# Turning three tiles on VectorE and through transfers instead of on TensorE, in a one-core decoder layer

## The chip, the core and the metric

The kernel runs on one core of a Trainium2 chip. A core has five engines that work side by side, each through its own queue of instructions in order: TensorE (PE in the profile, with its weight loads as PEld), VectorE (DVE), ScalarE (ACT), GpSimd (POOL) and SyncE (SP), whose queue here does little but issue transfers (DMAs) between the chip's memory and the core's. The metric is the time of one execution on the device in microseconds (us); lower is better. Of several executions the median counts.

## What is computed

One layer of a hybrid decoder over 256 tokens of width 1024, all in float32:

```python
def reference(x, ...):
    mix = hybrid_mixer(x, ...)
    x = layer_norm(ALPHA * x + mix, ln1_g, ln1_b)
    ffn = conv_gated_mlp(x, w_up, conv_ffn, w_down)
    return layer_norm(ALPHA * x + ffn, ln2_g, ln2_b)

def hybrid_mixer(x, ...):
    proj = x @ w_in + b_in                 # q,k,v,o,i,f of the memory; q,k,v of the attention; two gates
    qk = silu(causal_dwconv(concat(q_m, k_m), conv_qk))
    h_m = mlstm_chunkwise(q_m, k_m, v_m, i_m, f_m)          # 4 heads x 256
    y_a = sigmoid(o_m) * head_norm(h_m, mlstm_norm)
    y_b = moba_attention(q_b, k_b, v_b, rel_bias)           # 8 heads x 128
    merged = sigmoid(g_a) * (y_a @ w_branch_a) + sigmoid(g_b) * (y_b @ w_branch_b)
    return merged @ w_out

def conv_gated_mlp(x, w_up, conv_ffn, w_down):              # 2816 hidden columns
    g, up = split(causal_dwconv(x @ w_up, conv_ffn), 2)
    return (silu(g) * up) @ w_down
```

## The kernel before

**Chunks and slots.** All weights come as chunks of 128 x 2048 numbers (1 MB), in an order written out by hand in `chunk_order` (lines 45 to 58): four of the output gate, then for each of four groups of heads (g = 0 to 3) the chunks qm, qb, km, kb, vm, vb, ga, gb; then the branch chunks wa 0, wa 1, wb 0, wb 1, wa 2, wa 3, wb 2, wb 3; four chunks wo of the output projection; then the up chunks (22) and down chunks (11) of the MLP, mixed. A float32 product is made of three matmuls (`mm3`, line 143): every operand is split into a high part (ACT rounds it, line 94) and the rest (DVE subtracts, line 95). One chunk stands for 48 matmuls of 256 columns, or 24 of 512 for a down chunk.

**The loop** (lines 338 to 375) goes over the chunks; this text calls one turn of it, and the time of its matmuls, a slot. In slot s the code hands out, in this order: to ACT and DVE what is due (`elem_work`, line 381: the evacuation of the previous chunk's result, extra pieces from `side_elem`, and the split of chunk s+2, put between them where the list has a `None`; `mixed` can reorder the list); to SP the load of chunk s+5; to PE the matmuls of chunk s and then the pieces of `side_pe`. Every engine works its queue strictly in the order of the code. A tile that is given out again waits until all readers of its former content are done: raw chunks, high parts and low parts each have three buffers, and the results of the chunks share three banks of the accumulator memory (PSUM), "main", while five banks, "side", serve the rest.

**Groups.** In each group a head pair's memory output `yt` has tokens on the partitions and must be turned so that features are there (`yah`, `yal`: the operands of wa). For groups 0 to 2 `turn` (line 636) does this: DVE transposes 32 x 32 blocks into a spare tile, SP writes that to the chip's memory (line 644), and four loads bring it back (line 648); only then does `el_y` (line 755) split it. For the last group PE turns it: `pe_y` (line 748), four transposes at the end of slot gb 3, whose result in PSUM `el_y` reads. The two attention logits of a group are turned by `turn` in all four groups (`turn(0)` and `turn(1)`), cast by `el_t`, and used by `pe_o` (line 817); `el_o` (line 830) writes `ybh`, `ybl`, the operands of wb. For the last group `pe_o` stands at the end of slot wa 0 and `el_o` in slot wa 1.

**MLP.** The first two up chunks are multiplied with the tokens on the partitions (`step_up`, lines 1032 to 1047), since the second half of the tokens is normalised late. So their results have to be turned: `copy` brings them to `tu`, and `back` (line 1055), run by PE in the middle of chunk up 2, makes eight transposes into PSUM, `ps_upT`. `up_evac` (line 1076) is the evacuation of an up chunk: `conv` scales twice on ACT (line 1088) and adds two taps on DVE (line 1092, four instructions), `gate` applies Silu on ACT (line 1099), multiplies on DVE (line 1103) and splits into `hh` and `hl`. The evacuations of up 0, up 1 and up 2 are woven together (line 1073). Down chunk d needs the results of up chunks 2d and 2d + 1. Up chunks from number 6 on are split in one piece of 2048 columns, the others in two of 1024 (line 116).

Of the kernel before, what the change touches and what calls it, by code (L numbers as in the profile page):

```python
# [10 lines left out]
F32 = mybir.dt.float32  # L11
# [7 lines left out]
P = 128  # L19
S = 256  # L20
D = 1024
KT = D // P
# [22 lines left out]
def chunk_order():  # L45
# [7 lines left out]
    order += [("up", i) for i in range(4)]  # L53
    for d in range(8):
        order += [("dn", d), ("up", 2 * d + 4), ("up", 2 * d + 5)]
# [17 lines left out]
class Kernel:  # L73
# [69 lines left out]
    def mm3(self, ps, ah, al, bh, bl, start, stop, first=None, only=(0, 1, 2)):  # L143

        a = (ah if first is None else first, ah, al)
        b = (bh, bl, bh)
        for i in only:
            self.nc.tensor.matmul(ps, a[i], b[i], start=start and i == 0, stop=stop and i == 2)  # L148

# [30 lines left out]
    def run(self):  # L180
# [132 lines left out]
        for s, (kind, i) in enumerate(self.order):  # L313
            if kind == "qm":
# [5 lines left out]
        self.mrows = dram.tile([4, S], F32, name="mrows")  # L320
        self.flip = [[dram.tile([m, P, n * P], F32, name=f"flip{g}{i}")
                      for i, (m, n) in enumerate(((1, 3), (1, 3), (2, 2))[:3 if g < NG - 1 else 2])] for g in range(NG)]
# [15 lines left out]
        for s, (kind, i) in list(enumerate(self.order))[4:]:  # L338
# [3 lines left out]
            if s == first["wa"] + 1:  # L342
# [21 lines left out]
            parts = [] if late else self.split_parts(s + 2)  # L364
            if s == first["wa"] - 1:
                self.kept, parts = parts[-1], parts[:-1]
            self.elem_work(s, parts)
# [268 lines left out]
    def turn(self, t, d):  # L636
# [3 lines left out]
        tmp = self.ap.tile([P, 4 * P], F32, tag="turn", name="turn", bufs=2)[:, 0:n * P]  # L640
# [3 lines left out]
        self.nc.sync.dma_start(d.rearrange("m p f -> p m f"), tmp.rearrange("p (m f) -> p m f", m=m))  # L644
        t = t.rearrange("p c s -> p (c s)").rearrange("p (k f) -> p k f", k=4 * m)
# [4 lines left out]
    def group_schedule(self, g):  # L650
# [97 lines left out]
        def pe_y():  # L748
            psy = self.ps_side([P, 2, S], f"psy{g}")
            for j in range(2):  # L750
                for t in range(2):
                    nc.tensor.transpose(psy[:, j, t * P:(t + 1) * P], st["yt"][:, t, j * P:(j + 1) * P], self.ident)
            st["psy"] = psy

        def el_y():
            for j in range(2):
# [3 lines left out]
                if last:  # L760
                    y = st["psy"][:, j, :]
                else:
                    y = st["yt"].rearrange("p t s -> p (t s)").rearrange("p (m k) -> p m k", k=64)[:, :, 32 * j:32 * j + 32]
                    h, l = (t.rearrange("p (m i) -> p m i", i=32) for t in (h, l))
# [95 lines left out]
        self.mixed[b + 6 + o] = lambda w: ([lambda: el_l(1), lambda: el_e(1), el_n1] + w  # L860
                                           + [lambda: el_l2(1), el_n1b, lambda: turn(1)])
        if last:
            self.mixed[b + 7] = lambda w: [el_n2, lambda: el_t(0)] + w
            at(self.side_pe, 7, pe_y)
            self.mixed[b + 8] = lambda w: [el_y, self.kept, lambda: el_t(1)] + w
        else:
# [3 lines left out]
        at(self.side_pe, 8 + o, pe_o)  # L870
        at(self.side_elem, 9 + o, el_o)
# [19 lines left out]
    def step_wa(self, s, c, *a):  # L891
        nc = self.nc
        ps = self.ps_main(f"ps_wa{c}")
        self.mm_feat(s, ps, self.yah, self.yal)

        def evac():
            ga = self.sg["ga"][:, 2 * c:2 * c + 2, :]
            nc.scalar.activation(ga, ga, AF.Sigmoid)
            nc.vector.tensor_mul(ga, ps, ga)
        self.evac[s] = evac  # L900
# [126 lines left out]
    def step_up(self, s, i, *a):  # L1027
# [4 lines left out]
        if i < 2:  # L1032
# [17 lines left out]

            def copy():
                for j in range(2):
                    self.nc.scalar.copy(tu[:, j], self.pt_up[j])

            def back():
                for j in range(2):
                    ps = self.ps_side([P, 2, S], f"ps_upT{j}")
                    for f in range(2):
                        for t in range(2):
                            self.nc.tensor.transpose(ps[:, f, t * P:(t + 1) * P], tu[:, j, t, f * P:(f + 1) * P],  # L1060
# [260 lines left out]
```

## Time and profile before

| what | us |
|---|---|
| median of 3 runs | 479.17 |
| lowest, highest of them | 478.26, 479.36 |
| the execution that was profiled | 478.69 |
| its span, first to last instruction | 476.7 |
| DVE busy in the span | 368.1 |
| ACT busy in the span | 309.7 |
| bytes moved | 97.35 MB |

The profile is of one execution; its span is 2.0 us shorter than that execution's own time. In the lines shown below, a line of the timeline or of the chain has the start and the length in us, the engine, the line of the code and what it does; "[0.47 <-ACT hh]" says that the engine stood idle 0.47 us before it and what ended that. A group's line ends with the total busy time, and the mean of one in ns. Instructions on one engine overlap a little at their edges (the next starts some 0.1 us before the profile's end of the last), so the step from start to start is what counts where one engine is the limit.

### The profile page before, as it was taken

How to read it: one execution, taken by the hardware profiler on the slowest of the kernel's cores; microseconds unless marked ns; L12 is line 12 of the kernel's file. 1: busy time of each engine (PE TensorE's matmuls, PEld its weight loads, DVE VectorE, ACT ScalarE, POOL GpSimd, SP SyncE). 2: the span in 40 equal slices, each digit the busy share in tenths (PEclk: the TensorE clock that was granted, in tenths of full speed). 3: DMA queues.
4: the chain of work that ended last, by engine and by line, in shares of the span. 5: the costliest groups of instructions: out<-in, count | busy, mean ns of one | idle time of the engine just before them, and what ended most of it. 6: DMA issues, size and time to landing. Idle time of an engine off the chain costs nothing.

```text
span 476.7 us, 9493 instructions
## 1 busy us (share of the span) xinstructions
PE 469.3 (98%) x3788; PEld 454.8 (95%) x3788; DVE 368.1 (77%) x644; ACT 309.7 (65%) x540; POOL 37.4 (8%) x74
## 2 busy tenths in 40 slices
PE   8999999999999999999999999999999999999994
PEld 6999999999999999999999999999999999999984
DVE  4786979597869786986685898879668666778876
ACT  5669878597859786977663623765555545556871
POOL 0316501000200020010100001000000000000000
PEclk9999999999999999999999999999999999999999
DMA  7985665775666567655967472736564545456202
GB/s 232 324 298 180 212 239 162 222 276 195 173 239 247 193 171 253 234 169 177 368 243 260 148 294 88 268 101 252 184 236 170 206 178 192 171 214 219 89 0 89
DMA packets 28958, 97.35 MB, mean 204 GB/s; under 512 B 10581, under 2 KB 15585, under 8 KB 19697
## 3 DMA queue, kind: packets, MB, share of 16 engines
q1 hardware_dynamic: 27682, 92.51, 55.3%
q0 software_dynamic: 1232, 4.24, 2.7%
q8 instruction: 29, 0.48, 0.4%
q14 instruction: 15, 0.12, 0.1%
HBM read 93.31 MB, written 3.42 MB: 203 GB/s over the span
## 4 chain that ended last, share of the span: by engine, by line
PE 98%; DVE 0%; ACT 0%; DVEq 0%; issue 0%; ACTq 0%
PE ps_up L148 25%; PE ffn L148 13%; PE ps_ga L148 5%; PE ps_kb L148 5%; PE ps_vm L148 5%; PE mix L148 5%; PE ps_km L148 5%; PE ps_gb L148 5%; PE ps_wa L148 5%; PE ps_vb L148 5%; PE ps_wb L148 5%; PE ps_qm L148 5%; PE ps_qb L148 5%; PE ps_o0a L427 1%; PE ps_o0b L427 1%; PE psn L148 1%
## 5 line engine op out<-in xcount | busy, mean ns | idle before, releaser
L95 DVE TENSOR_TENSOR wl<-raw,wh 128x1024 fp32r<-128x1024 f32 (+4 forms) x147 | 180.0, 1261 | 26.8 <-ACT wh L94 24.5
L94 ACT CAST wh<-raw 128x1024 fp32r<-128x1024 f32 (+4 forms) x147 | 151.8, 1077 | 9.3 <-DMA raw<-in_wst_dram 4.0
L148 PE MATMUL ps_up<-x1h,wl 128*128 128x256 f32 x320 | 88.5, 276 | 0.0
L148 PE MATMUL ps_up<-x1h,wh 128*128 128x256 f32 x320 | 88.4, 276 | 0.0
L148 PE MATMUL ps_up<-x1l,wh 128*128 128x256 f32 x320 | 88.4, 276 | 0.0
L148 PEld LDWEIGHTS ps_up<-x1l,wh 128*128 128x128 f32 x320 | 60.1, 188 | 0.4
L148 PEld LDWEIGHTS ps_up<-x1h,wh 128*128 128x128 f32 x320 | 60.1, 188 | 0.3
L148 PEld LDWEIGHTS ps_up<-x1h,wl 128*128 128x128 f32 x320 | 60.1, 188 | 0.0
L1092 DVE SCALAR_TENSOR_TENSOR cu<-ps_up,vec,cu 128x255 f32<-128x255 f32 (+1 forms) x80 | 33.1, 476 | 20.1 <-ACT cu L1088 20.1
L148 PE MATMUL ffn<-wh,hl 128*128 128x512 f32 (+2 forms) x94 | 35.5, 378 | 0.0
L148 PE MATMUL ffn<-wl,hh 128*128 128x512 f32 (+2 forms) x94 | 35.5, 377 | 0.0
L148 PE MATMUL ffn<-wh,hh 128*128 128x512 f32 (+2 forms) x94 | 35.3, 375 | 0.0
L94 ACT CAST hh<-cu 128x256 fp32r<-128x256 f32 x22 | 8.9, 406 | 40.4 <-DVE cu L1103 40.4
L1088 ACT ACTIVATE cu<-ps_up,vec 128x256 f32<-128x256 f32 x40 | 16.7, 470 | 22.0 <-PE ps_up L148 22.0
L148 PEld LDWEIGHTS ffn<-wh,hl 128*128 128x128 f32 x94 | 17.7, 188 | 3.2
L148 PEld LDWEIGHTS ffn<-wl,hh 128*128 128x128 f32 x94 | 17.7, 188 | 3.1
L148 PEld LDWEIGHTS ffn<-wh,hh 128*128 128x128 f32 x94 | 17.7, 188 | 3.0
L990 POOL TENSOR_TENSOR rs<-rs,mhalf 128x1 f32<-128x1 f32 x3 | 2.1, 700 | 230.2 <-DVE rs L989 230.2
L148 PE MATMUL ps_ga<-xth,wh 128*128 128x256 f32 x64 | 18.0, 281 | 0.0
L148 PE MATMUL mix<-wh,mgh 128*128 128x256 f32 x64 | 17.8, 279 | 0.0
L148 PE MATMUL ps_wa<-yah,wh 128*128 128x256 f32 x64 | 17.8, 277 | 0.0
L148 PE MATMUL ps_kb<-xth,wl 128*128 128x256 f32 x64 | 17.7, 277 | 0.0
(344 smaller groups left out, 1476.6 us busy)
## 6 DMA issues: line engine op xcount, KB each, us to landing
raw<-in_wst_dram SPq DMA_DIRECT2D x72, 1024.0 KB, 4.9
raw<-in_wst_dram SPq DMA_DIRECT2D x10, 512.0 KB, 6.7
raw<-in_wst_dram SPq DMA_DIRECT2D x8, 256.0 KB, 4.5
lnrow<-in_rows_dram POOLq DMA_DIRECT2D x4, 512.0 KB, 6.9
flip<-turn SPq DMA_DIRECT2D x8, 192.0 KB, 3.2
lg<-flip SPq DMA_DIRECT2D x32, 48.0 KB, 2.0
xraw<-in_xt_dram SPq DMA_DIRECT2D x8, 128.0 KB, 4.0
toe<-table POOLq DMA_DIRECT2D x4, 256.0 KB, 4.7
```

The source lines that it names most:

```text
L94: self.nc.scalar.copy(wh, raw)
L95: self.nc.vector.tensor_sub(wl, raw, wh.bitcast(F32))
L148: self.nc.tensor.matmul(ps, a[i], b[i], start=start and i == 0, stop=stop and i == 2)
L427: mm(ps[t], x[:, k, t * P:(t + 1) * P], w, start=start and k == 0, stop=stop and k == KT - 1)
L990: nc.gpsimd.tensor_tensor(st["rs"], st["rs"], self.mhalf[:, 0:1], op=ALU.pow)
L1088: act.activation(cu[:, j, :], ps[:, j, :], AF.Copy, scale=tap(2, j))
L1092: v.scalar_tensor_tensor(cu[:, j, o:], ps[:, j, :S - o], tap(t, j), cu[:, j, o:], op0=ALU.mult, op1=ALU.add)
```

## The change

Three tiles are no longer turned by PE. The last group's `yt` goes the way of the other groups', through `turn(2)`, and `pe_y` is gone; the order of the last group's pieces over the slots ga, gb and wa 0 is written anew. Since `yt` and the second logits come back from memory in another order, the chunks wa 0 and wa 1 are cut: `mm_rows` runs wa 0 without its last two of eight row blocks (those that need group 3), then wa 1 without them, then the rest of wa 0, then `pe_o`, then the rest of wa 1; `el_o` and both evacuations of wa follow in slot wb 0. The results of up 0 and up 1 are copied to `tu`, turned by DVE into `tv`, written to memory and loaded back into `tu`; `natural` (two copies on ACT for each of the two chunks) brings the blocks into order, and `up_evac` reads `tv`. Their evacuations move to the slots up 4 and up 5. The order of the MLP chunks begins with up 0 to up 5, dn 1, dn 0, up 6, up 7 in place of up 0 to up 3, dn 0, up 4, up 5, dn 1, up 6, up 7; from dn 2 on it is as before.

```diff
--- before.py
+++ after.py
@@ -50,8 +50,8 @@
     for c in (0, 2):
         order += [("wa", c), ("wa", c + 1), ("wb", c), ("wb", c + 1)]
     order += [("wo", c) for c in range(4)]
-    order += [("up", i) for i in range(4)]
-    for d in range(8):
+    order += [("up", i) for i in range(6)] + [("dn", 1), ("dn", 0), ("up", 6), ("up", 7)]
+    for d in range(2, 8):
         order += [("dn", d), ("up", 2 * d + 4), ("up", 2 * d + 5)]
     order += [("up", 20), ("up", 21), ("dn", 8), ("dn", 9), ("dn", 10)]
     assert sum(k == "up" for k, _ in order) == NF and sum(k == "dn" for k, _ in order) == NF // 2
@@ -146,6 +146,14 @@
         b = (bh, bl, bh)
         for i in only:
             self.nc.tensor.matmul(ps, a[i], b[i], start=start and i == 0, stop=stop and i == 2)
+
+    def mm_rows(self, s, ps, xh, xl, ks):
+
+        wh, wl = self.w[s]
+        for j in range(2):
+            for k in ks:
+                a = self.col(s, k * 256 + j * P)
+                self.mm3(ps[j], wh[:, a:a + P], wl[:, a:a + P], xh[:, k, :], xl[:, k, :], k == 0, k == KT - 1)
 
     def mm_feat(self, s, ps, xh, xl, mid=None):
         wh, wl = self.w.pop(s)
@@ -318,8 +326,9 @@
 
         self.table = dram.tile([8, LTOE], F32, name="table")
         self.mrows = dram.tile([4, S], F32, name="mrows")
+        self.flip_up = [dram.tile([1, P, 4 * P], F32, name=f"flipu{j}") for j in range(2)]
         self.flip = [[dram.tile([m, P, n * P], F32, name=f"flip{g}{i}")
-                      for i, (m, n) in enumerate(((1, 3), (1, 3), (2, 2))[:3 if g < NG - 1 else 2])] for g in range(NG)]
+                      for i, (m, n) in enumerate(((1, 3), (1, 3), (2, 2)))] for g in range(NG)]
         self.gates_schedule(bif)
         self.gate_sums()
         self.rel_bias_expand(rel)
@@ -339,7 +348,7 @@
             if s == 10:
                 pre_cm.__exit__(None, None, None)
                 self.open_att(att_cm.__enter__())
-            if s == first["wa"] + 1:
+            if s == first["wa"] + 2:
                 self.elem_work(s)
                 att_cm.__exit__(None, None, None)
                 mix_cm.__exit__(None, None, None)
@@ -361,10 +370,7 @@
 
                 self.fp.tile([P, 24], F32, name="gap")
             late = s == first["up"]
-            parts = [] if late else self.split_parts(s + 2)
-            if s == first["wa"] - 1:
-                self.kept, parts = parts[-1], parts[:-1]
-            self.elem_work(s, parts)
+            self.elem_work(s, [] if late else self.split_parts(s + 2))
             self.load(s + 5)
             if s in (first["wo"], first["wo"] + 1):
                 self.split(s + 4)
@@ -633,15 +639,23 @@
         self.mixed[b + 2] = lambda w: w + [e1b, None, e1c, None, e1d, e1e]
 
 
-    def turn(self, t, d):
+    def turn(self, t, d, tmp=None):
 
         m, _, f = d.shape
         n, w = t.shape[1], t.shape[1] // m
-        tmp = self.ap.tile([P, 4 * P], F32, tag="turn", name="turn", bufs=2)[:, 0:n * P]
+        back = tmp is None
+        if back:
+            tmp = self.ap.tile([P, 4 * P], F32, tag="turn", name="turn", bufs=2)[:, 0:n * P]
         for k in range(m):
             self.nc.vector.transpose(tmp[:, k * f:(k + 1) * f].rearrange("p (b c i) -> p c b i", b=4, i=32),
                                      t[:, k * w:(k + 1) * w].rearrange("p c (b i) -> p c b i", b=4))
         self.nc.sync.dma_start(d.rearrange("m p f -> p m f"), tmp.rearrange("p (m f) -> p m f", m=m))
+        if back:
+            self.turn_in(t, d)
+
+    def turn_in(self, t, d):
+
+        m, _, f = d.shape
         t = t.rearrange("p c s -> p (c s)").rearrange("p (k f) -> p k f", k=4 * m)
         for b in range(4):
             src = d[:, :, b * (f // 4):(b + 1) * (f // 4)].rearrange("m (a j) f -> j m a f", a=4)
@@ -745,23 +759,13 @@
         def turn(i):
             self.turn(st["p", i] if i < 2 else st["yt"].rearrange("p t (j d) -> p (t j) d", j=2), self.flip[g][i])
 
-        def pe_y():
-            psy = self.ps_side([P, 2, S], f"psy{g}")
-            for j in range(2):
-                for t in range(2):
-                    nc.tensor.transpose(psy[:, j, t * P:(t + 1) * P], st["yt"][:, t, j * P:(j + 1) * P], self.ident)
-            st["psy"] = psy
-
         def el_y():
             for j in range(2):
                 c = 2 * g + j
                 gain = self.vec[:, V_NORM + c:V_NORM + c + 1]
                 h, l = self.yah[:, c, :], self.yal[:, c, :]
-                if last:
-                    y = st["psy"][:, j, :]
-                else:
-                    y = st["yt"].rearrange("p t s -> p (t s)").rearrange("p (m k) -> p m k", k=64)[:, :, 32 * j:32 * j + 32]
-                    h, l = (t.rearrange("p (m i) -> p m i", i=32) for t in (h, l))
+                y = st["yt"].rearrange("p t s -> p (t s)").rearrange("p (m k) -> p m k", k=64)[:, :, 32 * j:32 * j + 32]
+                h, l = (t.rearrange("p (m i) -> p m i", i=32) for t in (h, l))
                 a.activation(h, y, AF.Copy, scale=gain)
                 v.scalar_tensor_tensor(l, y, gain, h.bitcast(F32), op0=ALU.mult, op1=ALU.subtract)
 
@@ -857,18 +861,24 @@
         if g == 0:
             at(self.side_elem, 6, lambda: self.floor_exp())
         at(self.side_elem, 5 + o, lambda: turn(0))
-        self.mixed[b + 6 + o] = lambda w: ([lambda: el_l(1), lambda: el_e(1), el_n1] + w
+        if last:
+            self.mixed[b + 6] = lambda w: ([el_n1, el_n1b, lambda: el_l(1), el_n2, lambda: turn(2), None, None,
+                                            lambda: el_e(1)] + w + [lambda: el_l2(1), lambda: turn(1)])
+            self.mixed[b + 7] = lambda w: [lambda: el_t(0)] + w
+            self.mixed[b + 8] = lambda w: [el_y, lambda: el_t(1)] + w
+        else:
+            self.mixed[b + 7] = lambda w: ([lambda: el_l(1), lambda: el_e(1), el_n1] + w
                                            + [lambda: el_l2(1), el_n1b, lambda: turn(1)])
-        if last:
-            self.mixed[b + 7] = lambda w: [el_n2, lambda: el_t(0)] + w
-            at(self.side_pe, 7, pe_y)
-            self.mixed[b + 8] = lambda w: [el_y, self.kept, lambda: el_t(1)] + w
-        else:
             self.mixed[b + 8] = lambda w: [el_n2, lambda: el_t(0), lambda: turn(2)] + w
             self.mixed[b + 9] = lambda w: w[0:1] + [lambda: el_t(1)] + w[1:]
             at(self.side_elem, 10, el_y)
-        at(self.side_pe, 8 + o, pe_o)
-        at(self.side_elem, 9 + o, el_o)
+        if last:
+            self.last_o = pe_o
+            at(self.side_elem, 10, el_o)
+            self.mixed[b + 10] = lambda w: w[-1:] + w[:-1]
+        else:
+            at(self.side_pe, 9, pe_o)
+            at(self.side_elem, 10, el_o)
 
 
     def open_post(self, pp):
@@ -891,13 +901,28 @@
     def step_wa(self, s, c, *a):
         nc = self.nc
         ps = self.ps_main(f"ps_wa{c}")
-        self.mm_feat(s, ps, self.yah, self.yal)
-
-        def evac():
+        ps = [ps[:, j, :] for j in range(2)]
+        if c < 2:
+            ps[1] = self.ps_side([P, 2, 256], f"ps_wa{c}b")[:, 0, :]
+            self.mm_rows(s, ps, self.yah, self.yal, range(KT - 2))
+            if c == 0:
+                self.first_wa = s, ps, c
+                return
+            self.mm_rows(*self.first_wa[:2], self.yah, self.yal, range(KT - 2, KT))
+            self.last_o()
+        self.mm_rows(s, ps, self.yah, self.yal, range(KT - 2 if c < 2 else 0, KT))
+
+        def evac(s, ps, c):
             ga = self.sg["ga"][:, 2 * c:2 * c + 2, :]
             nc.scalar.activation(ga, ga, AF.Sigmoid)
-            nc.vector.tensor_mul(ga, ps, ga)
-        self.evac[s] = evac
+            for j in range(2):
+                nc.vector.tensor_mul(ga[:, j, :], ps[j], ga[:, j, :])
+        done = [(s, ps, c)]
+        if c == 1:
+            done.insert(0, self.first_wa)
+        for t in done:
+            self.w.pop(t[0])
+        self.evac[s] = [lambda t=t: evac(*t) for t in done]
 
     def step_wb(self, s, c, *a):
         nc = self.nc
@@ -1048,30 +1073,32 @@
             del self.w[s - 1], self.w[s]
             tu = self.fp.tile([P, 2, 2, S], F32, name="tu")
 
+            tv = self.fp.tile([P, 2, 2, S], F32, name="tv")
+
             def copy():
+                rows = [tu[:, j].rearrange("p t (f d) -> p (t f) d", f=2) for j in range(2)]
                 for j in range(2):
                     self.nc.scalar.copy(tu[:, j], self.pt_up[j])
-
-            def back():
                 for j in range(2):
-                    ps = self.ps_side([P, 2, S], f"ps_upT{j}")
-                    for f in range(2):
-                        for t in range(2):
-                            self.nc.tensor.transpose(ps[:, f, t * P:(t + 1) * P], tu[:, j, t, f * P:(f + 1) * P],
-                                                     self.ident)
-                    self.pt_up[j] = ps
+                    self.turn(rows[j], self.flip_up[j], tv[:, j].rearrange("p f s -> p (f s)"))
+                for j in range(2):
+                    self.turn_in(rows[j], self.flip_up[j])
+
+            def natural(j):
+                src = tu[:, j].rearrange("p t s -> p (t s)").rearrange("p (a t f i) -> p f t a i", a=4, t=2, f=2)
+                for f in range(2):
+                    self.nc.scalar.copy(tv[:, j, f].rearrange("p (t a i) -> p t a i", t=2, a=4), src[:, f])
+
             self.evac[s] = copy
-            self.back = back
-            self.up_parts = [self.up_evac(j, lambda j=j: self.pt_up[j]) for j in range(2)]
+            (a0, b0), (a1, b1) = [self.up_evac(j, lambda j=j: tv[:, j]) for j in range(2)]
+            self.side_elem.setdefault(s + 3, []).extend([lambda: natural(0), a0, b0])
+            self.mixed[s + 4] = lambda w: [lambda: natural(1), a1, b1, None, None] + w
+            self.mixed[s + 5] = lambda w: [None, None] + w
             return
         ps = self.ps_main(f"ps_up{i}")
-        self.mm_feat(s, ps, self.x1h, self.x1l, self.back if i == 2 else None)
+        self.mm_feat(s, ps, self.x1h, self.x1l)
         conv, gate = self.up_evac(i, lambda: ps)
-        parts = [conv, None, None, gate]
-        if i == 2:
-            (a0, b0), (a1, b1) = self.up_parts
-            parts = [a0, a1, conv, b0, None, None, b1, gate]
-        self.evac[s] = parts
+        self.evac[s] = [conv, None, None, gate]
 
     def up_evac(self, i, get_ps):
         v, act, pp = self.nc.vector, self.nc.scalar, self.fp
@@ -1111,7 +1138,7 @@
 
     def step_dn(self, s, d, *a):
         nc = self.nc
-        if d == 0:
+        if d == 1:
             self.st = [self.ln_tiles(f"2_{t}") for t in range(2)]
             a0 = [self.ps_side([P, 512], f"ffn0{h}") for h in range(2)]
             a1 = [self.ps_side([P, 512], f"ffn1{h}") for h in range(2)]
@@ -1126,12 +1153,12 @@
 
         d0 = NF // 2 - 3
 
-        def mm(dd, kk, t, ps, cols, fresh=0, more=False):
+        def mm(dd, kk, t, ps, cols, fresh=2, more=False):
             b = self.col(self.order.index(("dn", dd)), kk * D)
             w = [x[:, b + cols[0]:b + cols[1]] for x in self.w[self.order.index(("dn", dd))]]
             k = 2 * dd + kk
             hh, hl = (x[:, t * P:(t + 1) * P] for x in self.hid[k])
-            self.mm3(ps, hh, hl, w[0], w[1], k == fresh and not more, k == (2 * d0 if t and not fresh else NF) - 1)
+            self.mm3(ps, hh, hl, w[0], w[1], k == fresh and not more, k == (2 * d0 if t and fresh == 2 else NF) - 1)
 
         def part(t, q):
             ps, cols = self.acc[t][q]
```

## The prediction

> **What bounds the kernel now.** I read the page's first part and its chain first.
>
> ```profile
> PE 469.3 (98%) x3788; PEld 454.8 (95%) x3788; DVE 368.1 (77%) x644; ACT 309.7 (65%) x540; POOL 37.4 (8%) x74
> ...
> PE 98%; DVE 0%; ACT 0%; DVEq 0%; issue 0%; ACTq 0%
> ```
>
> PE is busy 98% of the span of 476.7 us and the chain that ended last runs through PE for 98% of it. So a matmul that goes saves its time on PE, and a new wait of PE costs its whole length; ACT and DVE have slack on average only. Next, PE's timeline where the two turns on PE stand:
>
> ```profile
> 219.90 0.28 PE L148 MATMUL ps_gb<-xth,wl 128*128 128x256 f32 x1
> 220.02 0.60 PE L752 MATMUL psy<-ident,yt 128*128 128x128 f32 x4
> 220.37 0.37 PE L148 MATMUL ps_wa<-yah,wh 128*128 128x256 f32 x1
> 220.58 0.28 PE L148 MATMUL ps_wa<-yal,wh 128*128 128x256 f32 x1
> ...
> 302.50 0.28 PE L148 MATMUL ps_up<-x1h,wl 128*128 128x256 f32 x1
> 302.63 1.03 PE L1060 MATMUL ps_upT<-ident,tu 128*128 128x128 f32 x8
> 303.42 0.36 PE L148 MATMUL ps_up<-x1h,wh 128*128 128x256 f32 x1
> 303.62 0.28 PE L148 MATMUL ps_up<-x1l,wh 128*128 128x256 f32 x1
> ```
>
> And the chain in order of time, whose pieces end when PE's results are there:
>
> ```profile
> 311.87 5.49 PE ffn L148 x24
> 317.36 10.89 PE ps_up L148 x96
> ```
>
> Two up chunks take 10.89 us for 96 matmuls, so one chunk is 5.44 us and the step from matmul to matmul 0.1134 us; a down chunk is 5.49.
>
> **What PE saves.** From the matmul before the four transposes to the second one behind them, 219.90 to 220.58, pass 0.68 us; two plain steps are 0.23, so 0.45 goes. Around the eight, 302.50 to 303.62 is 1.12 us, less 0.23 is 0.89. Together **-1.34 us**. The number of all other matmuls stays. Two changes fewer between up and down chunks are worth at most 2 x 0.05 (5.49 against 24 x 0.227 = 5.44); I take nothing for them.
>
> The Trainium skill speaks against the change: "VectorE: DVE Perf Modes", section "Rules for kernel authors", wants a 128 x 128 transpose on TensorE where the result may lie in PSUM. By this trace TensorE's price here is the 1.34 us above, and the question is what the other way makes late; that is the third rival.
>
> **The MLP's first chunks: what DVE and ACT then have to do.** The rows are of one up chunk's evacuation before, together with a split:
>
> ```profile
> 315.91 2.00 ACT L94 CAST wh<-raw 128x1024 fp32r<-128x1024 f32 x2
> 323.57 1.91 ACT L94 CAST wh<-raw 128x2048 fp32r<-128x2048 f32 x1
> 328.23 0.41 ACT L94 CAST hh<-cu 128x256 fp32r<-128x256 f32 x1 [2.44 <-DVE cu L1103]
> 328.54 0.83 ACT L1088 ACTIVATE cu<-ps_up,vec 128x256 f32<-128x256 f32 x2
> ...
> 324.01 1.65 DVE L1092 SCALAR_TENSOR_TENSOR cu<-ps_up,vec,cu 128x255 f32<-128x255 f32 x4
> 325.58 2.28 DVE L95 TENSOR_TENSOR wl<-raw,wh 128x2048 fp32r<-128x2048 f32 x1
> 329.41 1.65 DVE L1092 SCALAR_TENSOR_TENSOR cu<-ps_up,vec,cu 128x255 f32<-128x255 f32 x4 [0.32 <-ACT cu L1088]
> ```
>
> From taps to taps, 324.01 to 329.41, an up chunk holds DVE for 5.40 us, as long as PE needs for one (5.44). With a split in two pieces (ACT 2.00 in place of 1.91) it is some 5.55. So a row of up chunks runs at DVE's limit, and only down chunks give it air. What the turned chunks need on top has these nearest rows:
>
> ```profile
> L465 ACT ACTIVATE cvqm<-cbuf,vec 128x256 f32<-128x256 f32 x8 | 3.6, 508 | 0.0
> L94 ACT CAST pth<-lg 128x256 fp32r<-128x256 f32 x8 | 3.2, 398 | 1.1 <-DMA lg<-flip 1.1
> ...
> 213.29 0.58 DVE L642 STREAM_TRANSPOSE turn<-lg 128x384 f32<-128x384 f32 x1
> ...
> L642 DVE STREAM_TRANSPOSE turn<-yt 128x256 f32<-128x256 f32 x6 | 2.3, 418 | 0.0
> ```
>
> The two transposes of 512 columns, estimated 0.74 us each (0.58 for 384 plus 128 columns at 0.16), fall into slot up 2, before its result is there; DVE would be idle then: nothing. The transfers have from there to slot up 4, over 10 us. `natural` costs two copies at 0.40 a chunk, the scaling from SBUF 0.50 in place of 0.47. Both are new links ahead of the taps, since ACT reaches them only when the former chunk's `hh` is done.
>
> Now the queues, in before's clock. up 2's result came at 311.87 - 5.44 = 306.43 and comes 0.89 earlier, 305.54; the results of up 3, up 4, up 5, dn 1, dn 0 follow at 310.98, 316.43, 321.87, 327.36, 332.85. Taps of up 2 start at 305.54 + 0.84 (two scalings) = 306.4; taps of up 3 at 306.4 + 5.55 = 311.95; its `hh` on ACT ends at 316.75. Then `natural` 0 and two scalings, 4 instructions, about 1.1 until the first tap may go: 317.8; taps 1.57, then Silu, product and `hh` one after the other, each as long as the `hh` row, 0.03 between them (Silu may start at the third tap's end): ACT is free at 320.3. Chunk 1 the same, 3.6 later: taps at 321.4, ACT free at 324.0. Split of dn 0: ACT to 326.0, DVE from 325.05 to 327.5; dn 0's first part is ready at 326.3, in time for 327.4. Taps of up 4 at 327.4, `hh` done at 330.0; the high part of up 6 by ACT from 329.9 to 331.8; its low part by DVE 331.85 to **334.1**. PE starts up 6 at 332.85 less the 0.16 by which a matmul's issue is ahead of its end in the chain, and needs the low part in the third matmul, 332.9: **it waits 1.2 us**. Then DVE does the taps of up 5, `hh` ends at 336.7, ACT rounds up 7 until 338.5, DVE has the low part at **340.8**; PE, already 1.2 late, wants it at 339.6: **1.2 more**. The same addition for before, from 300.6 on, gives the end of up 6's low part as 327.99 where the row above ends at 325.58 + 2.28 = 327.86, so it leans 0.1 late: I take **+2.3** in all, with ends 1.7 (copies at 0.30, scaling 0.42) and 2.9 (copies at 0.50). Below that only if ACT or DVE does not follow the code's order. dn 2, next, gives DVE back what it lacks; up 8 is split 4 us ahead.
>
> **The branch chunks.** Rows for the last group:
>
> ```profile
> 210.45 0.40 ACT L802 ACTIVATE lg<-lg,mx 128x128 f32<-128x128 f32 x1 [2.24 <-DVE mx L795]
> 209.57 0.28 DVE L793 CUSTOM_DVE_ANT_0 lg<-psl,toe 128x128 f32<-128x128 f32 x1
> 210.32 0.76 DVE L715 BATCH_NORM_STATS2 bs<-psn 128x6 f32<-128x256 f32 x2
> 215.54 0.91 ACT L743 ACTIVATE yt<-yt,scl 128x256 f32<-128x256 f32 x2 [0.39 <-POOL scl L737]
> 229.32 0.47 ACT L835 ACTIVATE ybh<-pso,vec 128x256 fp32r<-128x256 f32 x1 [0.79 <-DVE ybl L836]
> ...
> 177.21 0.38 SPq L89 DMA_DIRECT2D raw<-in_wst_dram  x1
> 183.33 1.80 SPq L648 DMA_DIRECT2D yt<-flip  x4
> 186.90 0.91 ACT L765 ACTIVATE yah<-yt,vec 128x256 fp32r<-128x256 f32 x2 [2.84 <-DMA yt<-flip]
> 206.96 0.33 SPq L644 DMA_DIRECT2D flip<-turn  x1
> 208.87 2.62 SPq L648 DMA_DIRECT2D lg<-flip  x4
> 211.58 0.38 SPq L89 DMA_DIRECT2D raw<-in_wst_dram  x1
> ```
>
> A turned tile is written some 6.1 us after the raw load issued ahead of it (177.21 to 183.33, behind which its loads may go) or 1.9 us after its own issue with nothing ahead (206.96 to 208.87), and is back 3.6 us after its first load (183.33 to 186.90). The statistics now go first, at 209.57 in place of 210.32, and `yt` is scaled by about 214.0 to 214.9 (0.75 earlier, and 0.8 for work no longer between). DVE turns it by 215.75, it is written at 217.7 and back at 221.3. Ahead of the second logits' turn ACT now has the split of wa 0 (2.0), so their exponentials start at 216.9; before, from exponentials to the end of the turn passed 3.4 (210.45 to 213.87): turned at 220.4, written at 222.5 (1.9 and a little for the `yt` loads ahead), back at **226.1**. Without `psy`, wa 0 starts at 220.0; wa 1 at 224.1 (36 steps), the rest of wa 0 at 228.2, `pe_o` at 229.5, wb 0 at 232.1. `yah` is done near 225: three us ahead. `el_t`, the gate (1.5 together) and wb 0's split (ACT 2.0, DVE 1.26 behind) end at 231, its first piece in time for 232.3. wb 1's split takes the buffer of wa 0, free at 229.8 only: DVE 230.9 to 233.3; behind it `el_o`, which goes ACT, DVE, ACT, DVE (0.48 each, as 229.32 shows it waiting for DVE) to 235.1 at most, 234.8 likely. PE needs the last piece at 232.1 + 21 steps + 0.11 = 234.6: **+0.2**, ends 0 and 3.3 (third rival). The evacuation of wa 0 behind it leaves its bank an estimated 1 us before wb 1 needs it. SP issues five DMAs more in slot ga and ten in up 2, 0.45 each (1.80 for four), and waits there until the written tile has landed, so the weight loads queued behind go some 5 and 7 us later. A chunk is loaded five slots and split two slots ahead of its matmuls, so a load has three slots, 16 us, and nothing waits for it.
>
> **Sum:** -1.34 + 2.3 + 0.2 = **+1.2 us**. Against the profiled execution's 478.69 that is 479.9; the median of the runs is 0.48 higher, 480.4. I say **480.2**. Under 0.3% (1.44 us) this measurement cannot tell from no change.
>
> **Rivals.** (1) *Nothing new ends last*: ACT and DVE keep ahead; -1.3, 477.8. For it: DVE is at 77%, and the transfers are early. Against: the 5.40 us row and before's sum, right to 0.1. Chance 0.20. (2) *Half*: up 6 is split in time and only up 7 is late, or copies are cheap; about +0.1, 479.3. Chance 0.13. (3) *The branch hand-off is late, slower than before*: second logits back at 229.3 because their write goes behind a load (6.1 instead of 2.2). From 226.3 on, each us late passes through `el_t`, wb 0's split and `el_o` to PE: +3.1 on top, 483.4. Against: no load lies ahead of it in SP's queue. Chance 0.12. The rule of the Trainium skill quoted above ("VectorE: DVE Perf Modes", "Rules for kernel authors") would have the time come out on this side; in before ACT stands idle for such a transfer (2.84 us, row 186.90) but PE never, so it gets no more than that chance. (4) *The change doesn't remove PE's work*: excluded, the transposes are gone from the code.
>
> **How the numbers follow.** My forecast has 0.55, its own range 479.4 to 481.2, of which 0.30 lies within 0.3% and 0.25 above. Rival 1: 0.05 faster by over 0.3%, 0.15 within. Rival 2 within, rival 3 slower. So faster 0.05, same 0.58, slower 0.37. The range 477.5 to 482.0 takes in rivals 1 and 2 and the upper ends, and leaves most of rival 3 out.
>
> **What would show it.** Right: no `psy` and `ps_upT` on PE; PE idle about 1.2 us in up 6 and in up 7, ended by DVE's low part; 0 to 0.5 us in wb 0, ended by `ybl`. Wrong: no idle time on PE in up 6 (my DVE sum fails), or one in wa 0 to wb 0 of over 1 us (the transfers).

## The result, and the profile after

Of 22 executions each, the kernel before has a median of 478.66 us and the changed kernel of 481.8 (479.75 to 485.85). The ratio is 1.0072, with a 95% interval of 1.0058 to 1.0085: **about 3.4 us slower**. The profiled execution happens to be the slowest of the 22, 485.85 us with a span of 484.1. So a second one was profiled (below: "second look", 480.62 us, span 478.9), and the two are read side by side.

The page's first lines of the changed kernel, busy time and the chain's shares:

```profile
PE 472.6 (98%) x3776; PEld 456.5 (94%) x3776; DVE 370.1 (76%) x652; ACT 311.4 (64%) x544; POOL 36.3 (7%) x74
...
PE 63%; ACT 14%; DVE 12%; DMA 6%; issue 3%; POOL 1%; SPq 1%; DVEq 0%; ACTq 0%; POOLq 0%
```

PE has twelve instructions less and is busy for the same 98% of the span, but the chain that ended last ran through PE for 98% and now does so for 63%. The share is that of one execution: in the second look it is 91%. In the first, most of what PE lacks lies between 87 and 201 us, ahead of every slot that the change edits, where the chain goes through transfers of turned tiles, ACT and DVE. What the new code makes PE wait for is read from PE's timeline. Its columns are start, length, engine, line, operation, and in brackets PE's idle time and what ended it:

```profile
221.22 0.28 PE L148 MATMUL ps_gb<-xth,wl 128*128 128x256 f32 x1
221.34 0.28 PE L148 MATMUL ps_wa<-yah,wh 128*128 128x256 f32 x1
...
235.44 0.28 PE L148 MATMUL ps_wb<-ybh,wh 128*128 128x256 f32 x1
236.97 0.38 PE L148 MATMUL ps_wb<-ybl,wh 128*128 128x256 f32 x1 [1.25 <-DVE ybl L840]
...
237.47 0.38 PE L148 MATMUL ps_wb<-ybh,wh 128*128 128x256 f32 x1
237.99 0.39 PE L148 MATMUL ps_wb<-ybl,wh 128*128 128x256 f32 x1
...
338.21 0.28 PE L148 MATMUL ps_up<-x1l,wh 128*128 128x256 f32 x1
339.69 0.39 PE L148 MATMUL ps_up<-x1h,wl 128*128 128x256 f32 x1 [1.20 <-DVE wl L95]
339.91 0.28 PE L148 MATMUL ps_up<-x1h,wh 128*128 128x256 f32 x1
...
345.15 0.28 PE L148 MATMUL ps_up<-x1l,wh 128*128 128x256 f32 x1
346.41 0.38 PE L148 MATMUL ps_up<-x1h,wl 128*128 128x256 f32 x1 [0.98 <-DVE wl L95]
346.63 0.28 PE L148 MATMUL ps_up<-x1h,wh 128*128 128x256 f32 x1
```

Between ps_gb and ps_wa there is a plain step now, with no `psy`. PE waits in wb 0 and in up 6 and up 7. The same places in the second look:

```profile
235.19 0.38 PE L148 MATMUL ps_wb<-ybl,wh 128*128 128x256 f32 x1
235.41 0.28 PE L148 MATMUL ps_wb<-ybh,wl 128*128 128x256 f32 x1
...
333.18 0.28 PE L148 MATMUL ps_up<-x1l,wh 128*128 128x256 f32 x1
334.65 0.39 PE L148 MATMUL ps_up<-x1h,wl 128*128 128x256 f32 x1 [1.20 <-DVE wl L95]
...
340.10 0.28 PE L148 MATMUL ps_up<-x1l,wh 128*128 128x256 f32 x1
341.37 0.39 PE L148 MATMUL ps_up<-x1h,wl 128*128 128x256 f32 x1 [1.00 <-DVE wl L95]
```

The two MLP waits are the same in both. In wb 0 only a step of 0.22 in place of 0.11 is left. With the starts of stages on PE in the three profiles (us), the differences become a balance:

| stage begins | before | after | second look | after less before | second look less before |
|---|---|---|---|---|---|
| ps_ga of the last group | 209.12 | 210.44 | 209.72 | +1.32 | +0.60 |
| ps_wb (wb 0) | 232.53 | 233.40 | 232.69 | +0.87 | +0.16 |
| ps_wa (wa 2) | 243.41 | 248.14 | 243.69 | +4.73 | +0.28 |
| mix (wo 0) | 265.18 | 269.91 | 265.46 | +4.73 | +0.28 |
| ps_up (up 0) | 287.85 | 293.20 | 288.16 | +5.35 | +0.31 |
| dn 2 | 344.47 | 351.93 | 346.73 | +7.46 | +2.26 |

The first row arose ahead of the edited slots. From ps_ga to ps_wb both lose the 0.45 us of the four transposes. From up 0 to dn 2 both pay about 2 us (2.11 and 1.95). Between them stands wb 0 with wb 1: 3.86 us dearer in the one execution, 0.12 in the other. So the change has a loss in the MLP that both profiles show alike, and one in the branch that only one of them shows.

For the one in the MLP, the rows of DVE in the first profile, as in the prediction's sum:

```profile
337.34 2.29 DVE L95 TENSOR_TENSOR wl<-raw,wh 128x2048 fp32r<-128x2048 f32 x1 [1.38 <-ACT wh L94]
...
344.06 4.56 DVE L95 TENSOR_TENSOR wl<-raw,wh 128x2048 fp32r<-128x2048 f32 x3 [1.39 <-ACT wh L94]
```

The low part of up 6 is done at 337.34 + 2.29 = 339.63, and PE goes on at 339.69. The second row starts with the low part of up 7, done 2.29 later at 346.35; PE goes on at 346.41. For the other one, DVE and ACT in the same profile (DVE's rows first):

```profile
231.89 4.63 DVE L95 TENSOR_TENSOR wl<-raw,wh 128x1024 fp32r<-128x1024 f32 x4 [1.45 <-ACT wh L94]
236.44 0.48 DVE L840 SCALAR_TENSOR_TENSOR ybl<-pso,vec,ybh 128x256 fp32r<-128x256 f32 x1
```

```profile
229.57 0.41 ACT L94 CAST pth<-lg 128x256 fp32r<-128x256 f32 x1 [4.02 <-DMA lg<-flip]
```

The second logits are back from memory only when the cast of `pth` starts, at 229.57. Behind it ACT and DVE do four half splits (wb 0's and wb 1's) and then `ybl`, in the order of the code. In the second look the same cast starts here:

```profile
226.77 0.41 ACT L94 CAST pth<-lg 128x256 fp32r<-128x256 f32 x1 [3.84 <-DMA lg<-flip]
```

**Why 2.8 us later?** The SP rows of the two profiles, the first and then the second look: group 2's turned `yt` is written, and the loads that bring it back go when it has landed.

```profile
178.54 0.38 SPq L652 DMA_DIRECT2D flip<-turn  x1
185.98 1.79 SPq L662 DMA_DIRECT2D yt<-flip  x4
```

```profile
176.54 0.38 SPq L652 DMA_DIRECT2D flip<-turn  x1
182.64 1.79 SPq L662 DMA_DIRECT2D yt<-flip  x4
```

It took 7.44 us in the one and 6.10 in the other, and it starts 2.0 us apart, since the logits' write ahead of it in the same queue took 5.2 us in the one and 3.4 in the other. The chain of the first profile goes on from there, through ACT and DVE, to a wait of PE near 201 us:

```profile
178.54 7.37 DMA flip<-turn
189.52 0.52 ACT yah L769
201.51 0.74 PE pss L148 x4
```

The rest of the hand-off moves with it, as seven profiles of kernels with the new branch part show (us):

| loads of group 2's `yt` issued | 181.28 | 181.76 | 182.58 | 182.64 | 184.90 | 185.23 | 185.98 |
|---|---|---|---|---|---|---|---|
| last group's second cast of `pth` | 223.8 | 226.3 | 226.0 | 226.8 | 227.7 | 227.6 | 229.6 |

The write of that `yt` took 5.6 to 7.4 us in them, and 5.6 to 6.2 in the four profiles with the old branch chunks. Group 2's code is the same in both; whether the longer times there are chance is open. That the two rows of the table move together is what seven profiles show; the way from the one to the other was not followed step by step.

### The profile page after: what moved, and what is told of

Same layout as the page of the kernel before. It is cut to its first block, busy times and chain, and to the rows that moved or that the text cites. A ratio compares the mean times of both kernels' runs of the same rounds, so it can differ in the third digit from the quotient of the medians.

```text
span 484.1 us, 9515 instructions
## 1 busy us (share of the span) xinstructions
PE 472.6 (98%) x3776; PEld 456.5 (94%) x3776; DVE 370.1 (76%) x652; ACT 311.4 (64%) x544; POOL 36.3 (7%) x74
## 4 chain that ended last, share of the span: by engine, by line
PE 63%; ACT 14%; DVE 12%; DMA 6%; issue 3%; POOL 1%; SPq 1%; DVEq 0%; ACTq 0%; POOLq 0%
PE ps_up L148 20%; PE ffn L148 10%; DVE wl L95 6%; ACT wh L94 6%; PE ps_wa L148 3%; PE ps_wb L148 3%; DMA flip<-turn 3%; PE mix L148 2%; PE ps_vb L148 2%; PE ps_ga L148 2%; PE ps_gb L148 2%; PE ps_qb L148 2%; PE ps_qm L148 2%; DVE cu L1119 2%; DMA yt<-flip 2%
## 5 line engine op out<-in xcount | busy, mean ns | idle before, releaser
L148 PE MATMUL ps_wb<-ybl,wh 128*128 128x256 f32 x64 | 18.7, 292 | 1.4 <-DVE ybl L840 1.2
L148 PE MATMUL ps_wb<-ybh,wh 128*128 128x256 f32 x64 | 18.5, 289 | 0.0
L148 PE MATMUL ps_wb<-ybh,wl 128*128 128x256 f32 x64 | 18.4, 288 | 0.0
L148 PE MATMUL mix<-wl,mgh 128*128 128x256 f32 x64 | 17.8, 278 | 0.3 <-DVE wl L95 0.3
```

## The experiments

Each kernel is compared with the kernel before on the same chip; the ratio is given with its 95% interval. The edits are shown against the changed kernel.

**The two halves alone.** The branch part with the old MLP, and the MLP part with the old branch chunks.

```diff
-    order += [("up", i) for i in range(6)] + [("dn", 1), ("dn", 0), ("up", 6), ("up", 7)]
-    for d in range(2, 8):
+    order += [("up", i) for i in range(4)]
+    for d in range(8):
...
+            self.back = back
+            self.up_parts = [self.up_evac(j, lambda j=j: self.pt_up[j]) for j in range(2)]
```

> The part on the branch chunks alone; the MLP as before. Theory: PE saves 0.45 us (psy) and loses more in wb 0, where ybl of the last head stands behind wb 1's split on DVE, together with a stretch at low clock behind that wait: +0.5 to +2 us in all, ratio 1.001 to 1.004, a wait of PE in wb 0 of 0.2 to 1.5 us ended by ybl. Rival (the loss comes from the MLP part alone, or from the transfers' load on all queues): -0.4 to 0 us, ratio 0.999 to 1.000, no wait in wb 0.

Measured: 479.84 (478.25 to 483.08), ratio 1.0028 (1.0008 to 1.0048). The ratio is as the theory had it, but the profile (of an execution of 479.01) doesn't show the theory's wait. The logits are back early, and ACT even stands still until PE has read wa 0's weights, whose buffer wb 1's split takes:

```profile
223.80 0.41 ACT L94 CAST pth<-lg 128x256 fp32r<-128x256 f32 x1 [1.94 <-DMA lg<-flip]
...
229.17 2.00 ACT L94 CAST wh<-raw 128x1024 fp32r<-128x1024 f32 x2 [2.13 <-PE ps_wa0b L148]
```

In wb 0 a single step is longer, 0.20 us. This execution loses 1.25 us from wb 0 to wb 3 by longer steps of PE, of which the last section tells.

```diff
+            at(self.side_pe, 7, pe_y)
...
-        if last:
-            self.last_o = pe_o
-            at(self.side_elem, 10, el_o)
...
+        at(self.side_pe, 8 + o, pe_o)
+        at(self.side_elem, 9 + o, el_o)
```

> The part on the MLP's first chunks alone, with its order of up and down chunks; the branch as before. Theory: the waits of PE in up 6 and up 7 (1.2 and 1.0 us idle, about 2.7 with the slower steps behind them) less 0.89 saved: +1.8 us, ratio 1.004, both waits ended by DVE's low part. Rival (a stretch at low clock follows these waits too in some executions): +2.5 to +4, ratio 1.005 to 1.008, and the granted clock below that of before.

Measured: 480.79 (479.6 to 481.8), ratio 1.0044 (1.0031 to 1.0057). Its profile has both waits, 1.22 us in up 6 and 1.01 in up 7. The two losses, 0.28% and 0.44%, add to the 0.72% of the whole change, within intervals of 0.1 to 0.2%. The MLP's times are narrow, the branch's wide, as in the balance.

**The MLP's waits.** First, the gate of up 4 is handed out behind the split of up 6:

```diff
-            self.mixed[s + 4] = lambda w: [lambda: natural(1), a1, b1, None, None] + w
-            self.mixed[s + 5] = lambda w: [None, None] + w
+            held = []
+            def up4(w):
+                held.append(w[-1])
+                return [lambda: natural(1), a1, b1, None, None] + w[:-1]
+            self.mixed[s + 4] = up4
+            self.mixed[s + 5] = lambda w: [None, None] + held + w
```

> As the MLP part alone, but the gate of up 4 is handed out behind the split of up 6. Theory (only the order of DVE's and ACT's work makes PE wait): no wait in up 6 and up 7, -0.9 us, ratio 0.998. Rival (the turned chunks or their transfers come too late whatever the order): a wait of over 0.5 us stays in dn 0, up 6 or up 7, ratio 1.001 or more.

Measured: 478.98 (478.76 to 479.68), ratio 1.0006 (0.9994 to 1.0018); more was expected. Its PE timeline says what is left: up 6 runs through, and up 7 still waits, 1.18 us.

```profile
338.63 0.28 PE L148 MATMUL ps_up<-x1l,wh 128*128 128x256 f32 x1
340.09 0.38 PE L148 MATMUL ps_up<-x1h,wl 128*128 128x256 f32 x1 [1.18 <-DVE wl L95]
```

The gate of up 5 still stood ahead of the split of up 7, on both engines. With it behind that split too (`hold` takes the last piece of the list, the gate, and keeps it in `held`):

```diff
...
+            self.mixed[s + 4] = lambda w: [lambda: natural(1), a1, b1, None, None] + hold(w)
+            self.mixed[s + 5] = lambda w: [None, None, held.pop()] + hold(w)
+            self.mixed[s + 6] = lambda w: [None, None, held.pop()]
```

> MLP part alone, with gate 4 behind the split of up 6 and gate 5 behind the split of up 7. Theory A (PE's two waits in up 6 and up 7 are the gates of up 4 and up 5 standing ahead of the splits on ACT and DVE; the first mend took away one of them, and the trace kept 1.18 us in up 7): both waits gone, low part of up 7 done 1 us before PE wants it; 1.3 to 1.5 us less than the first mend, ratio 0.9970 to 0.9982, median about 477.4. Rival (DVE is at its limit over the whole row of up chunks, so the wait only moves on): a new wait of 0.5 us or more in dn 2 to up 9, ratio 0.999 to 1.001.

Measured: 477.56 (477.03 to 478.84), ratio **0.9981** (0.9972 to 0.9990). PE has no wait in up 6 or up 7: in the chain the two take 10.89 us, as two up chunks did before. DVE does the low part of up 7 at 334.37, and PE starts up 7 at about 337.9:

```profile
332.60 10.89 PE ps_up L148 x96
```

```profile
334.37 2.29 DVE L95 TENSOR_TENSOR wl<-raw,wh 128x2048 fp32r<-128x2048 f32 x1
```

So DVE was not short of time over the row of up chunks; two pieces stood in the wrong place in its queue. That accounts for the MLP's loss: 1.0044 with both pieces ahead, 1.0006 with one, 0.9981 with none.

**The branch part's order.** wb 1's split behind `el_o` instead of ahead of it, with the old MLP:

```diff
-            self.elem_work(s, [] if late else self.split_parts(s + 2))
+            parts = [] if late else self.split_parts(s + 2)
+            if s == first["wa"] + 1:
+                self.kept, parts = parts, []
+            self.elem_work(s, parts)
...
-            self.mixed[b + 10] = lambda w: w[-1:] + w[:-1]
+            self.mixed[b + 10] = lambda w: w[-1:] + self.kept + w[:-1]
```

> As the branch part alone, but the split of wb 1 is handed out behind el_o. Theory (el_o is late because it stands behind that split): the wait ended by ybl goes, -0.4 us, ratio 0.999. Rival (the turned logits come back too late, so pe_o itself is late): a wait of 0.5 us or more stays, in pe_o or in wb 0, and the ratio stays above 1.001.

Measured: 478.59 (477.71 to 481.21), ratio 1.0009 (0.9990 to 1.0027). In its profile PE has no wait in wb 0, though the logits are back at 227.6 only. The ratio lies between the theory's and the rival's. Six of its twelve executions lie at 477.7 to 478.2, but four at 480.3 to 481.2. Next, wb 0 by rows as well, so that PE needs `ybl` 18 matmuls later:

```diff
-        self.mm_feat(s, ps, self.ybh, self.ybl)
+        ps = [ps[:, j, :] for j in range(2)]
+        if c == 0:
+            ps[1] = self.ps_side([P, 2, 256], f"ps_wb{c}b")[:, 0, :]
+            self.mm_rows(s, ps, self.ybh, self.ybl, range(KT - 2))
+        self.mm_rows(s, ps, self.ybh, self.ybl, range(0 if c else KT - 2, KT))
...
```

> Branch part alone, el_o ahead of wb 1's split, and wb 0 by rows (k 0 to 5 of both halves first), so PE reads the last group's ybh/ybl some 16 steps (1.8 us) later than in the branch part with el_o first. Theory A (the scatter of 477.7 to 481.2 us there comes from the second logits' return through DRAM, which landed at 223.8, 227.6 and 229.6 us in three profiles): wb 0 then tolerates a return until about 230.5 and pe_o until about 230.0, so nearly every execution is a fast one: median about 478.0, ratio 0.998 to 1.000, highest below 479.5, no wait of PE in wb 0 ended by ybl. Rival B (the scatter comes from group 2's late yt, which delays pss near 200 us and which this edit doesn't touch): as before the edit, median about 478.6, ratio 1.000 to 1.003, highest above 480.5.

Measured: 478.89 (477.69 to 480.02), ratio 1.0006 (0.9996 to 1.0017). The highest time fell from 481.2 to 480.0, as the theory of the late logits had it, though not below its 479.5; the median did not fall, and there it was wrong. Its profile shows one more place where PE stops, in wo 3. The weight loads' rows of PE (PEld), then ACT's:

```profile
276.17 0.19 PEld L148 LDWEIGHTS mix<-wl,mgh 128*128 128x128 f32 x1 [0.20 <-DVE wl L95]
```

```profile
271.63 2.09 ACT L94 CAST aheadh<-raw 128x256 fp32r<-128x256 f32 x3 [2.31 <-DMA raw<-in_wst_dram]
```

Before wo 3's split ACT has to round up 0's weights, and waits 2.31 us for them to arrive; in the kernel before it is 1.29. The chain of waits of the changed kernel's first profile runs through the same place, from the transfer to PE:

```profile
270.18 6.54 DMA raw<-in_wst_dram
277.13 0.84 ACT aheadh L94
...
280.08 1.23 DVE wl L95
281.36 8.34 PE mix L148 x71
```

**The return made later.** A direct test of the late logits: the changed kernel, with the last group's second logits written twice, the second write behind the first. PE, ACT and DVE have nothing more to do.

```diff
-        self.nc.sync.dma_start(d.rearrange("m p f -> p m f"), tmp.rearrange("p (m f) -> p m f", m=m))
+        for _ in range(n_w):
+            self.nc.sync.dma_start(d.rearrange("m p f -> p m f"), tmp.rearrange("p (m f) -> p m f", m=m))
...
+                      n_w=2 if last and i == 1 else 1)
```

> The changed kernel with the last group's second logits written twice to DRAM, the second write behind the first, so they are back about 2 us later and no engine does more. Theory A (the branch loss hangs on this return: free until 226.7, then 1 us per us): the cast of pth about 228.5 to 231, PE's wait in wb 0 ended by ybl 1.5 to 4 us, and the median 2 to 4 us above the changed kernel's 481.8, ratio to the kernel before 1.010 to 1.016. Rival B (the loss is el_o's place behind wb 1's split or group 2's late yt, and the return has slack): wait in wb 0 below 0.5 us, ratio 1.006 to 1.009 as without.

Measured, of four executions: 484.85 (481.23 to 488.13), ratio 1.0127 (1.0081 to 1.0172). ACT's row of the cast, and PE's:

```profile
229.41 0.41 ACT L94 CAST pth<-lg 128x256 fp32r<-128x256 f32 x1 [4.51 <-DMA lg<-flip]
```

```profile
236.81 0.39 PE L148 MATMUL ps_wb<-ybl,wh 128*128 128x256 f32 x1 [1.20 <-DVE ybl L842]
```

The first write is issued at 221.62 and the loads at 225.55, 3.9 us later; in the changed kernel's first profile it was 2.2. Group 2's `yt` was late in this execution too, its loads at 185.47, so this profile is like the first one; the evidence is the median, which rose by 3 us over the changed kernel's for 2 us of lateness. The ratio is the theory's; with four executions the interval begins at 1.0081 and just touches the rival's 1.006 to 1.009. The second look shows the other end:

> The changed kernel once more, for a second profile beside the first, which was its slowest execution (485.85 us). Theory A (the branch loss depends on when the second logits are back, the MLP loss doesn't): waits of 1.1 to 1.3 us in up 6 and in up 7 as in the first; the cast of pth ended by the transfer between 223.5 and 229.6 us, and the wait in wb 0 is near zero if it is before 226.3 and grows 1 us per us behind it; time 479.7 to 482.5 us. Rival B (the wait in wb 0 doesn't depend on it): about 1.2 us in wb 0 whatever the landing.

Measured: 480.62, the return at 226.77, 0.11 us in wb 0, and 1.20 and 1.00 us in up 6 and up 7.

**All mends together.** The whole change with `el_o` first, wb 0 by rows, and both gates behind the splits (the edits above):

> The whole change with both mends (el_o first, wb 0 by rows, gates 4 and 5 behind the splits). Theory A: the losses of the change are these waits and nothing else, so what is left is PE's saving: ratio 0.9960 to 0.9980, median about 476.9, no wait of PE in wb 0, up 6 or up 7, highest below 479. Rival B (late transfers of group 2, or more traffic, cost what the mends can't give back): ratio 0.999 to 1.002 and a scatter above 3 us.

Measured: 477.76 (477.03 to 479.18), ratio 0.9983 (0.9974 to 0.9992), between the theory and the rival, and without a wait of PE in wb 0, up 6 or up 7 in its profile. And with up 0's and up 1's splits one slot later, behind wo 3's:

```diff
-            if s in (first["wo"], first["wo"] + 1):
-                self.split(s + 4)
+            if s in (first["wo"] + 1, first["wo"] + 2):
+                self.split(s + 3)
```

> The whole change with both mends, and the two ahead splits (up 0, up 1) each one slot later, behind wo 3's split. In the branch part by rows PE had a pause of 0.18 + 0.11 us at wo 3's first low part, since on ACT wo 3's split stands behind up 0's, which waits for its weights (2.31 us there, 1.29 in the kernel before), and behind it steps of 0.118 instead of 0.113 us. Theory A (this is where the branch part's 0.45 us from the turn goes): no pause in wo 3, 0.2 to 0.5 us less than both mends without it (0.9983), ratio 0.9970 to 0.9982. Rival B (the pause is only one execution's): same as without, 0.998 to 0.999.

Measured: 477.57 (476.81 to 479.95), ratio 0.9979 (0.9962 to 0.9996). The two intervals and that of the MLP part alone (0.9981) overlap, and the profile without this last edit has no pause in wo 3 either, so whether wo 3's place costs the median anything is not settled. Three versions are about 1 us faster than the kernel before, and the simplest leaves the branch chunks as they were: the MLP part with its two gates moved.

## Why the prediction was wrong

The forecast was 480.2 with 479.4 to 481.2 as its own range; 481.8 lies above that, just inside the wide one, and slower by more than the 0.3% had 0.37 against 0.58 for the same. The base was a little off too: 479.17 was the median of three executions, and of 22 it is 478.66.

**PE's saving** was right: 0.45 us from ps_ga to ps_wb in both profiles, and with both gates moved the MLP is 0.66 us shorter from up 0 to dn 2 (55.96 against 56.62), with 0.14 of the 0.89 lost to longer steps in up 0 (4.95 against 4.81), which two profiles with the old MLP have as well.

**The MLP's waits** were right in place, cause and time: 1.2 and 1.0 us idle in up 6 and up 7, ended by DVE's low part, against 1.2 and 1.2. The term was mis-sized otherwise: a wait costs more than its idle time. From start to start, up 6's matmul took 1.47 us in the second look and the next one 0.22, where two plain steps are 0.23: 1.46 us. With 1.26 in up 7 that is 2.7 in place of 2.3.

**The branch term** is the step that failed: "+0.2, ends 0 and 3.3". As a sum for one execution it held: the second look's logits are back at 226.8 where 226.1 was worked out, and wb 0 and wb 1 lose 0.12. But the sum took one profile's transfer times as the kernel's. The hand-off's price was given in rival 3 (free until 226.3, which is 5.8 us ahead of its wb 0, then 1 us per us). In the first profile the return is 3.8 us ahead of wb 0, so 2.0 late, and PE lost 2.2 in pauses: that price was right. The other 1.6 of the 3.9 is a stretch at half the clock behind the pauses (last section), for which the prediction had no term.

What was wrong is that rival's chance, 0.12, and its argument against, that no load lies ahead of the second logits' write. None does. The lateness is there 40 us earlier, in group 2's writes behind weight loads in the same queue, and the return moves with it. With the old branch chunks the loads of the second logits go at 215.8 to 217.4 in four profiles, with the new ones at 220.5 to 225.1 in seven: later, behind the write and the loads of `yt`, and with the room used up that they had before anyone needed them. So the term is a spread behind a threshold and not one price, and its median was +1.4 us (branch part alone against before) in place of the forecast -0.25. Lateness is not all of it: in the branch part's own profile the return was 7.8 us ahead of wb 0, and wb 0 to wb 3 still lost 1.25 us by longer steps. Only profiled executions show the return, so how the +1.4 divides between the two stays open.

**"Nothing waits for it"**, of the delayed weight loads, was wrong in a smaller way: `aheadh` waits for them, and wo 3's split behind it. In the first profile the stage wo cost 0.62 us more than before.

Together, by the ratios of the halves: the MLP part cost 2.1 us where 2.3 less 0.89, 1.4, was forecast, the branch part 1.3 where it was -0.25. These 0.7 and 1.6 over a sum of +1.2 make 3.5; measured were 3.4. Of the MLP's 0.7 the price of the waits is 0.4; the rest is not assigned. The figure named as a refutation, over 1 us in wa 0 to wb 0, occurs in the first profile and not in the second.

The Trainium skill's rule against the change ("VectorE: DVE Perf Modes", "Rules for kernel authors": a 128 x 128 transpose belongs on TensorE if the result may lie in PSUM) came out for the last group's `yt`: taking it off TensorE gained nothing that could be measured, even with the mends. For up 0 and up 1 the measurement decides the other way: 0.9981 once the queue was put in order.

## What to carry to other kernels

A profile shows one execution: before work is moved behind a transfer, look at how far that transfer's landing moves between executions, and ask what the change leaves of its slack. When an evacuation is moved to another slot, put the next chunk's split ahead of whatever is not yet needed; two reordered pieces were worth 3 us here, more than the eight transposes. And count a wait of TensorE with the steps behind it, not by its idle time.

## What was not expected of the hardware

**Behind pauses of 2.2 us together the granted clock was half.** The windows of the changed kernel's first profile (stretch, its length, busy time and instructions of PE, PEld, DVE, ACT and POOL, the granted clock, the transfers' share, GB/s), and below them one of the kernel with the double write:

```profile
236.00:239.00 3.00, 1.89 (x11) 1.49 (x12) 1.40 (x3) 2.02 (x3) 0.00 (x0) 1.00 1.02 388
239.00:242.60 3.60, 3.60 (x20) 3.60 (x19) 3.17 (x6) 3.30 (x5) 0.00 (x0) 0.53 0.97 366
```

```profile
237.80:241.00 3.20, 3.17 (x15) 3.17 (x16) 1.73 (x5) 3.19 (x5) 0.00 (x0) 0.50 1.03 364
```

In wb 0 PE lost 2.2 us between 235.44 and 238.22, and then ran 16 steps of 0.21 us in place of 0.11: 1.6 us of the 3.9. No such stretch follows the waits of 1.20 and 0.98 us in up 6 and up 7, which lie 6.7 us apart. The Trainium skill ("TensorE: Matmul & The Clock Gate", "Why this matters for your kernels") asks for no idle gap above about 3 us; here half the clock came behind a gap of 1.25 us (1.20 in the other profile) with smaller ones beside it. How large the pauses must be was not tried. The length of the slow stretch, 3.2 to 3.4 us, agrees with the window of 3.4 us in that page's "Part 1".

**Stretches of longer steps at full clock.** In the branch part alone the only pause in wb 0 is one step of 0.20, at 234.11. Its chain of waits, two chunks a line, and the second look's below:

```profile
231.78 11.29 PE ps_wb L148 x96
243.07 11.31 PE ps_wa L148 x96
254.38 11.31 PE ps_wb L148 x96
```

```profile
232.85 11.00 PE ps_wb L148 x96
243.85 10.88 PE ps_wa L148 x96
254.73 10.89 PE ps_wb L148 x96
```

The step is 0.118 instead of 0.113 us for 31 us, at a granted clock of 1.00: 1.3 us in all. The profile of the kernel with all mends and the later splits shows the same behind two steps of 0.19 and 0.23 us in wb 0, for 47 us, into wo; the second look, with a step of 0.22, doesn't. But the same steps occur in group 0, which no edit touches. The second look's chain there, and the kernel before's:

```profile
70.16 5.65 PE ps_gb L148 x48
```

```profile
70.19 5.45 PE ps_gb L148 x48
```

Three chunks in a row take 5.65 us in the second look, 0.6 us more than before: that is its +0.60 in the first row of the balance. So whether the pause brings the longer steps is not shown, and what does was not tried. They may be why mending the branch part narrowed its times more than it lowered them, but that is only argued.
